# Forming the low parts of layer 1's k, q and v weights during layer 0's feed-forward and keeping them in DRAM scratch

## The chip, the cores and the metric

One core of a Trainium2 chip. The metric is the device time of one execution in microseconds; the kernel before has three runs, 1903.14, 1904.91 and 1908.84, with a median of 1904.91 us.

## The reference

One inference step of a two-layer decoder for a prompt of 512 tokens and 8 sample tokens, 520 columns in all, of width D = 1024, in float32. Layer 0 mixes with dilated-window attention and an SSM, layer 1 with a gated delta net; each is followed by a SwiGLU feed-forward of width 2816, and each of the four sub-layers stands between two RMS norms. The change is about one product, the input projection of layer 1 (8192 + 32 columns: q 1024, k 1024, v 2048, which pass a causal convolution and silu, z 2048, and gates):

```python
def gdn_mixer(h, conv_buf, s0, w_in, conv_w, dt_bias, a_log, norm_w, w_out):
    proj = h @ w_in
    qkv, z, b_raw, a_raw = jnp.split(proj, [GDN_QKV, GDN_QKV + GDN_VW, ...], axis=-1)
    qkv, new_conv = causal_conv(qkv, conv_buf, conv_w)
    qkv = jax.nn.silu(qkv.astype(f32))
    ...
    o, s_fin = gated_delta_rule(q, k, v, g, beta, s0)
    ...
def swiglu(h, w_gate, w_up, w_down):
    return (jax.nn.silu(h @ w_gate) * (h @ w_up)) @ w_down
```

The outputs also hold the updated states and caches. The sample caches come back with every row moved up by one, which the kernel does with 32 copies of 1 MB from DRAM to DRAM.

## The kernel before

**Products.** Activations lie feature-major: 128 features on the partitions, 520 tokens in two halves of 256 and 264. TensorE multiplies float32r operands, so each weight tile W is split into a high part (W rounded by a cast) and a low part (W minus the high part), and so is each activation x. A product is hi·xh + hi·xl + lo·xh: three matmuls for each 128 × 128 weight tile and token half, six for both halves (`lin`).

**Weights.** `WStream.load` brings raw weights into a ring of two buffers of 1 MB, for the input projections and feed-forward gate and up 8 row tiles × 256 columns, so two column tiles a load (the out-projection of layer 0: 12 row tiles × 128 columns, 768 KB). `WStream.split` then works in units of four row tiles × 128 columns: a cast of 128 × 512 into a buffer `whi` (L289 on ACT, L290 where DVE or POOL does it), and a subtraction into `wlo` (L165). Each of the two rings has four units. `s.lo_pool` chooses the engine of the subtraction at each stage: POOL for every unit, or for every second or third, DVE for the others.

**Order.** A scheduler decides the order of instructions on each of the five engines, with priorities; on the chip each engine then takes its own list strictly in order, and waits on semaphores. SP issues nearly all DMAs (L296), so its list is also the order in which transfers enter its queue. `copy_after` hangs one cache copy behind every `copy_every`-th weight load: every 4th in layer 0 and layer 1, none for the z columns and the output projection of layer 1, every 2nd in the last feed-forward; what is left goes at the end.

**Stages.** Layer 0's input projection and mixers; its out-projection (`w_hyb_out`; the last column tiles are computed by token halves, all first halves before the second); the boundary (residual and norm: DVE and ACT, PE works on the feed-forward's first tiles as the norm's parts arrive); feed-forward 0, whose gate and up run over 11 pairs of column tiles and down over 22 row tiles; boundary; layer 1 from about 840 us on. In layer 1, `l1` computes the gates and k tiles, the elimination systems of the delta rule, q tiles and v tiles. Each of the 32 tiles passes `conv_tile`: a scale from PSUM, four steps of a convolution (L281 `cs<-cs,cw` on DVE, others on ACT and POOL `cs<-cs,p`), silu (L281 `p<-p,cs`). The elimination (`l1_eliminate`, products `p<-p,b` and `b<-p` on DVE with both inputs in SBUF) runs between them; the scheduler mixes the two.

Names that are needed below: `raw`, `whi`, `wlo` (the rings), `cs` and `b4` (two large SBUF buffers that each stage uses for other things), `gqd0` and `gqd1` (queries of layer 1 kept in DRAM and loaded back to `b4` four at a time), `ktd` (keys kept likewise), `acc` (PSUM accumulators), `ma` and `mb` (other PSUM).

Of the kernel before, what the change touches and what calls it, by code (L numbers as in the profile page):

```python
# [28 lines left out]
EPS = 1e-6  # L29
# [91 lines left out]

def KN(n, v, *others):
    """The engine, share or order chosen at a place: v unless the table has another of the choices."""
    return KNOBS.get(n, v)
# [4 lines left out]
class WStream:  # L129
    """Weights, in the order of use: loaded in groups, split into hi + lo in units of at most 4 row tiles."""  # L130

    def __init__(s, k):
        s.k, s.ng, s.nu, s.nh = k, 0, 0, 0
        s.raw = s.key = None

# [12 lines left out]
    def split(s, raw, ko, nk, off, spread=None, out=None):  # L148
# [7 lines left out]
        with k.tc.high_priority():  # L156
# [3 lines left out]
            for o, d, n in spread or [(off, 0, 128)]:  # L160
                s.nh += 1
                k.cp("V" if k.hi_v and s.nh % k.hi_v == 0 else "A", hi[:, :nk, d:d + n], raw[:, :, o:o + n])
                s.nu += 1
# [5 lines left out]
    def tile(s, ap, c0, kts, spread=None, ncol=None, out=None):  # L169
        """Yield (row tile, hi, lo) for the 128 columns from c0 and the row tiles kts; input weights come two tiles a load.  # L170
        out = (buffer, offset) of 1024 floats for each four row tiles, to hold them apart from the ring."""
# [7 lines left out]
        for k0 in range(0, len(kts), 4):  # L179
            hi, lo = s.split(raw, kts[k0], 4, off, spread, out and out[k0 // 4])  # L180
            for j in range(4):
                yield kts[k0] + j, hi[:, j], lo[:, j]

    def rows(s, ap, c0, loads):
        """As tile() for a tall matrix; loads are (first row tile, count, unit offsets in their order)."""
# [9 lines left out]
class Ker:  # L195
# [14 lines left out]
    def gen(s, *names):  # L210
        """From here on these buffers hold something else: float32r operands and float32 data never share a tile."""
# [3 lines left out]
    def lay(s, name, off=0, n=KD, dt=F32R):  # L215
        """Operand (tile, half) -> columns, for n tiles of all tokens."""
# [3 lines left out]
    def layh(s, name, n=KD):  # L220
        """As lay(), the first half of the tokens of every tile before the second."""
# [64 lines left out]
    def cp(s, e, out, in_):  # L286
        """Copy on ACT, DVE or GpSimd."""
# [10 lines left out]
    # ---- linear layers: weights stationary, 520 token columns moving in two halves  # L298
    def lin(s, w, xh, xl, nkt, halves=(0, 1), ps=None):
        """ps[half] = sum over row tiles of w (yielding (row tile, hi, lo)) of hi'xh + hi'xl + lo'xh."""  # L300
# [7 lines left out]
    def group(s, w, xh, xl, nkt):  # L308
        """Up to four tiles, the first half of the tokens of all before the second half, which may come later."""
# [13 lines left out]
    def lnexp(s, ins):  # L323
        """After ins, one table load for Ln and Exp."""
# [1561 lines left out]
```

## Time and profile before

The profiled execution has a span of 1901.6 us; the runs are 1.5 to 7.2 us above that (median 3.3).

| stage, window in us | PE busy | DVE | ACT | POOL | granted clock |
| --- | --- | --- | --- | --- | --- |
| gate norm of layer 0 and before, 300 to 363 | 53.66 of 63 | 38.62 | 35.25 | 24.46 | 0.95 |
| out-projection of layer 0, 363 to 425 | 61.64 of 62 | 29.38 | 33.66 | 20.38 | 1.00 |
| boundary, start of feed-forward 0, 425 to 480 | 49.53 of 55 | 46.81 | 29.79 | 27.10 | 0.88 |
| feed-forward 0, 560 to 640 | 80.00 of 80 | 24.36 | 21.23 | 36.13 | 1.00 |
| layer 1, 870 to 900 | 26.66 of 30 | 26.40 | 17.41 | 19.23 | 1.00 |
| layer 1, 950 to 1000 | 30.98 of 50 | 49.58 | 26.57 | 36.13 | 0.84 |
| layer 1, 1200 to 1250 | 50.00 of 50 | 39.66 | 27.37 | 26.08 | 1.00 |

A busy PE is a TensorE that has a matmul in work; matmuls are pipelined, so this is not the same as full use. Each engine's column is the time in which it executed something. PE's clock falls where PE idles. A row of groups gives the line, the engine, the operation, output and inputs by name, shape, count, the group's busy time, the mean of one in ns, and the idle time of the engine before them with what ended it. A row of the chain gives a start, a duration and what the chain ran through there.

### The profile page before, as it was taken

How to read it: one execution, taken by the hardware profiler on the slowest of the kernel's cores; microseconds unless marked ns; L12 is line 12 of the kernel's file. 1: busy time of each engine (PE TensorE's matmuls, PEld its weight loads, DVE VectorE, ACT ScalarE, POOL GpSimd, SP SyncE). 2: the span in 40 equal slices, each digit the busy share in tenths (PEclk: the TensorE clock that was granted, in tenths of full speed). 3: DMA queues.
4: the chain of work that ended last, by engine and by line, in shares of the span. 5: the costliest groups of instructions: out<-in, count | busy, mean ns of one | idle time of the engine just before them, and what ended most of it. 6: DMA issues, size and time to landing. Idle time of an engine off the chain costs nothing.

```text
span 1901.6 us, 36269 instructions
## 1 busy us (share of the span) xinstructions
PE 1746.8 (92%) x14263; PEld 1659.2 (87%) x14263; DVE 1190.0 (63%) x2334; ACT 748.7 (39%) x1828; POOL 876.2 (46%) x768
## 2 busy tenths in 40 slices
PE   8899999898999999988968898989889999999996
PEld 7888777698999999977857787978889899999996
DVE  6898878638323221178899977888954954443125
ACT  5432335555222223355756555544334511111222
POOL 2565756234444433435474554646668411112452
PEclk9999999998999999999988899999989899999998
DMA  7345765453333334453442123257998333432333
GB/s 259 125 130 183 237 202 142 145 182 113 111 111 112 112 106 136 124 177 114 137 139 72 59 65 92 63 156 212 272 290 237 132 135 134 134 133 84 92 92 106
DMA packets 293323, 268.88 MB, mean 141 GB/s; under 512 B 11841, under 2 KB 276742, under 8 KB 291986
## 3 DMA queue, kind: packets, MB, share of 16 engines
q1 hardware_dynamic: 292502, 265.90, 45.5%
q8 instruction: 112, 1.84, 0.4%
q10 hardware_dynamic: 652, 0.68, 0.1%
q14 instruction: 57, 0.47, 0.1%
HBM read 241.01 MB, written 62.04 MB: 159 GB/s over the span
## 4 chain that ended last, share of the span: by engine, by line
PE 56%; DVE 26%; DMA 8%; issue 4%; ACT 4%; POOL 2%; SPq 1%; DVEq 0%; POOLq 0%; ACTq 0%
PE acc L268 48%; DVE p L274 4%; DVE cs L281 4%; PE ma L268 4%; PE mb L268 3%; DVE b L274 2%; DVE sq L281 2%; DMA raw<-in_w_ffn_down_dram 2%; DVE p L281 1%; DVE Hh L281 1%; PE mb L271 1%; DVE cs L274 1%; DMA bm<-csd 1%; POOL cs L274 1%; DVE wlo L165 1%
## 5 line engine op out<-in xcount | busy, mean ns | idle before, releaser
L165 POOL TENSOR_TENSOR wlo<-raw,whi 128x512 fp32r<-128x512 f32 (+3 forms) x373 | 500.8, 1346 | 676.7 <-ACT whi L289 368.1
L268 PE MATMUL acc<-Hl,whi 128*128 128x256 f32 (+1 forms) x2576 | 565.6, 291 | 20.2 <-DVE Hl L281 8.5
L268 PEld LDWEIGHTS acc<-Hl,whi 128*128 128x128 f32 x2576 | 420.5, 193 | 35.4 <-issue 11.3
L289 ACT CAST whi<-raw 128x512 fp32r<-128x512 f32 (+3 forms) x392 | 234.4, 602 | 453.0 <-PE acc L268 388.2
L268 PE MATMUL acc<-Hh,whi 128*128 128x256 f32 (+1 forms) x1824 | 387.0, 287 | 3.5 <-DVE cs L274 2.0
L268 PE MATMUL acc<-Hh,wlo 128*128 128x256 f32 (+1 forms) x1824 | 389.0, 288 | 0.0
L268 PEld LDWEIGHTS acc<-Hh,whi 128*128 128x128 f32 x1824 | 292.5, 191 | 8.2 <-issue 5.1
L268 PEld LDWEIGHTS acc<-Hh,wlo 128*128 128x128 f32 x1824 | 292.8, 191 | 7.5 <-issue 6.7
L268 PE MATMUL acc<-bm,whi 128*128 128x256 f32 (+1 forms) x1136 | 237.1, 290 | 1.4 <-DVE bm L281 1.4
L268 PE MATMUL acc<-p,whi 128*128 128x264 f32 (+1 forms) x1280 | 230.6, 287 | 4.4 <-ACT p L1819 1.6
L290 DVE CAST whi<-raw 128x512 fp32r<-128x512 f32 x131 | 61.1, 467 | 256.7 <-PE acc L268 195.2
L165 DVE TENSOR_TENSOR wlo<-raw,whi 128x512 fp32r<-128x512 f32 (+1 forms) x150 | 117.5, 785 | 142.2 <-ACT whi L289 138.8
L268 PEld LDWEIGHTS acc<-p,whi 128*128 128x128 f32 x1280 | 190.6, 192 | 6.4 <-ACT p L1819 1.9
L268 PEld LDWEIGHTS acc<-bm,whi 128*128 128x128 f32 x1136 | 182.1, 193 | 3.7 <-issue 1.6
L268 PE MATMUL acc<-p,wlo 128*128 128x256 f32 (+1 forms) x704 | 164.4, 288 | 8.7 <-DVE wlo L165 7.0
L268 PE MATMUL acc<-Hl,wlo 128*128 128x256 f32 (+1 forms) x752 | 171.1, 293 | 1.0 <-POOL wlo L165 0.9
L268 PEld LDWEIGHTS acc<-Hl,wlo 128*128 128x128 f32 x752 | 126.4, 195 | 3.2 <-POOL wlo L165 1.6
L268 PEld LDWEIGHTS acc<-p,wlo 128*128 128x128 f32 x704 | 119.6, 192 | 10.1 <-DVE wlo L165 7.9
L281 DVE SCALAR_TENSOR_TENSOR cs<-cs,cw 128x512 f32<-128x512 f32 x100 | 96.4, 966 | 12.7 <-POOL cs L274 8.6
L268 PE MATMUL acc<-X,whi 128*128 128x264 f32 (+1 forms) x512 | 100.4, 291 | 1.7 <-DVE X L274 1.3
L268 PEld LDWEIGHTS acc<-X,whi 128*128 128x128 f32 x512 | 80.4, 195 | 3.2 <-DVE X L274 1.6
L281 DVE SCALAR_TENSOR_TENSOR Hh<-cs,CS,Hh 128x256 f32<-128x256 f32 x64 | 53.1, 894 | 26.5 <-POOL Hh L274 26.2
(465 smaller groups left out, 2932.6 us busy)
## 6 DMA issues: line engine op xcount, KB each, us to landing
raw<-in_w_gdn_in_dram SPq DMA_DIRECT2D x24, 1024.0 KB
raw<-in_w_ffn_gate_dram SPq DMA_DIRECT2D x22, 1024.0 KB
raw<-in_w_ffn_up_dram SPq DMA_DIRECT2D x22, 1024.0 KB
raw<-in_w_ffn_down_dram SPq DMA_DIRECT2D x20, 1024.0 KB
raw<-in_w_hyb_in_dram SPq DMA_DIRECT2D x16, 1024.0 KB
out_sv_dram<-in_cache_attn_v_dram SPq DMA_DIRECT2D x16, 1023.0 KB
out_sk_dram<-in_cache_attn_k_dram SPq DMA_DIRECT2D x16, 1023.0 KB
raw<-in_w_gdn_out_dram SPq DMA_DIRECT2D x10, 1024.0 KB
```

The source lines that it names most:

```text
L165: eng.tensor_tensor(out=lo[:, :nk, d:d + n], in0=raw[:, :, o:o + n], in1=hi[:, :nk, d:d + n].bitcast(F32), op=ALU.subtract)
L268: s.nc.tensor.matmul(out, lhsT=lhsT, rhs=rhs, start=start, stop=stop, skip_group_check=skip)
L271: s.nc.tensor.transpose(out, in_, s.ident[0:in_.shape[0], 0:in_.shape[0]])
L274: return (eng or s.nc.vector).tensor_tensor(out=out, in0=a, in1=b, op=op).ins
L281: return s.nc.vector.scalar_tensor_tensor(out=out, in0=a, scalar=sc, in1=b, op0=op0, op1=op1).ins
L289: return s.nc.scalar.copy(out, in_).ins
L290: return (s.nc.vector if e == "V" else s.nc.gpsimd).tensor_copy(out, in_).ins
```

## The change

In the feed-forward of layer 0 a list `todo` of 60 units is set up: 30 of the 32 k, q and v column tiles of `w_gdn_in` (k tiles 2 to 7, q 0 to 7, v 0 to 15, each in two units of four row tiles). `park` takes one unit: SP loads its 256 KB of raw weights into one of two places in `cs`, ACT casts it into one of two places in `b4`, POOL subtracts in place, SP stores the 256 KB result to a scratch tile `pk0` to `pk59` in DRAM. Three units are asked for after each pair of tiles; the rest (27) after the loop. In layer 1 `split` finds such a unit by its key: the cast to `whi` stays, but `wlo` is loaded from scratch by a DMA in place of the subtraction. No cache copies are hung behind the loads of feed-forward 0; they start again with layer 1. The products themselves are the same.

```diff
+PARK = 3
+PTILES = [*range(10, 16), *range(8), *range(16, 32)]
 class WStream:
     def __init__(s, k):
         s.raw = s.key = None
+        s.parked, s.todo = {}, []
...
-    def split(s, raw, ko, nk, off, spread=None, out=None):
+    def park(s, n=1):
+        k = s.k
+        for _ in range(min(n, len(s.todo))):
+            ap, c0, k0 = s.todo.pop(0)
+            q = len(s.parked)
+            raw, lo = k.B("cs", 1040 + 512 * (q % 2), 4, 128), k.B("b4", 2080 + 512 * (q % 2), 4, 128, dt=F32R)
+            k.dma(raw, ap[k0 * 128:(k0 + 4) * 128, c0:c0 + 128].rearrange("(k p) c -> p k c", p=128))
+            k.cp("A", lo, raw)
+            k.tt(lo, raw, lo.bitcast(F32), ALU.subtract, k.nc.gpsimd)
+            d = k.dr.tile([128, 4, 128], F32, tag="pk%d" % q, name="pk%d" % q)
+            k.dma(d, lo.bitcast(F32))
+            s.parked[ap.tensor.name, ap.offset, c0, k0] = d
+
+    def split(s, raw, ko, nk, off, spread=None, out=None, low=None):
...
                 k.cp("V" if k.hi_v and s.nh % k.hi_v == 0 else "A", hi[:, :nk, d:d + n], raw[:, :, o:o + n])
+                if low is not None:
+                    k.dma(lo.bitcast(F32), low)
+                    continue
                 s.nu += 1
                 eng = nc.gpsimd if (k.lo_pool and s.nu % k.lo_pool == 0) else nc.vector
...
-            hi, lo = s.split(raw, kts[k0], 4, off, spread, out and out[k0 // 4])
+            hi, lo = s.split(raw, kts[k0], 4, off, spread, out and out[k0 // 4], s.parked.get((ap.tensor.name, ap.offset, c0, kts[k0])))
...
     def ffn(s, l):
         s.gen("p2" if l == 0 else "bm")
+        if l == 0:
+            w = s.i["w_gdn_in"][0]
+            s.copy_every = 0
+            s.W.todo = [(w, 128 * t, k0) for t in PTILES for k0 in (0, 4)]
...
                     s.tt(hl(t, h), gt, a.bitcast(F32), ALU.subtract)
+                if l == 0:
+                    s.W.park(PARK)
+        s.W.park(1000)
...
     def l1(s):
+        s.copy_every = KN('cev0', 4, 3, 5, 6)
```

In the built programs POOL has 52 subtractions of L165 fewer and 60 `b4<-cs,b4` more, DVE 8 subtractions fewer, ACT 60 casts more, SP 180 DMAs more; PE has the same instructions. Lines of the kernel are 22 further down after the change (L318 is the old L296, L187 the old L165). The scheduler puts the units not only into feed-forward 0: the first two loads stand before the end of layer 0's attention samples, units 0 to 19 are stored during the out-projection, 20 to 27 around the boundary.

SP's list in the second half of layer 0's out-projection, before (`raw` is the weight load of a column tile, `out_sv` and `out_sk` a cache copy):

```order
L296 DMA raw_4530<-in_w_hyb_out_dram 128x12x128
L296 DMA raw_4585<-in_w_hyb_out_dram 128x12x128
L296 DMA out_sv_dram<-in_cache_attn_v_dram 16x16368
L296 DMA raw_4641<-in_w_hyb_out_dram 128x12x128
L296 DMA raw_4740<-in_w_hyb_out_dram 128x12x128
```

The same place after the change, from `raw_4585` on (`cs_78` is a unit's raw weights, `pk12` its scratch tile):

```order
L318 DMA raw_4585<-in_w_hyb_out_dram 128x12x128
L318 DMA out_sv_dram<-in_cache_attn_v_dram 16x16368
L318 DMA pk12_5796<-b4_5014 128x512
L318 DMA cs_78<-in_w_gdn_in_dram 128x4x128
L318 DMA pk13_5801<-b4_5014 128x512
L318 DMA cs_78<-in_w_gdn_in_dram 128x4x128
L318 DMA raw_4641<-in_w_hyb_out_dram 128x12x128
L318 DMA pk14_5806<-b4_5014 128x512
L318 DMA cs_78<-in_w_gdn_in_dram 128x4x128
L318 DMA pk15_5877<-b4_5014 128x512
L318 DMA raw_4740<-in_w_hyb_out_dram 128x12x128
```

The weight loads of the out-projection now stand behind stores, which wait for POOL, and loads, which wait for the place in `cs`.

SP's list in feed-forward 0, before:

```order
L296 DMA raw_5538<-in_w_ffn_gate_dram 128x8x256
L296 DMA raw_5668<-in_w_ffn_up_dram 128x8x256
L296 DMA raw_5802<-in_w_ffn_gate_dram 128x8x256
L296 DMA raw_5932<-in_w_ffn_up_dram 128x8x256
L296 DMA out_sv_dram<-in_cache_attn_v_dram 16x16368
```

And after:

```order
L318 DMA raw_5597<-in_w_ffn_gate_dram 128x8x256
L318 DMA pk28_6470<-b4_5014 128x512
L318 DMA cs_78<-in_w_gdn_in_dram 128x4x128
L318 DMA pk29_6475<-b4_5014 128x512
L318 DMA cs_78<-in_w_gdn_in_dram 128x4x128
L318 DMA pk30_6678<-b4_5014 128x512
L318 DMA cs_78<-in_w_gdn_in_dram 128x4x128
L318 DMA pk31_6683<-b4_5014 128x512
L318 DMA cs_78<-in_w_gdn_in_dram 128x4x128
L318 DMA raw_5727<-in_w_ffn_up_dram 128x8x256
```

Four stores and four loads now stand between two weight loads, up to unit 59.

SP's list at the end of layer 1's v tiles, before (the last `raw` loads of v and the first of z; `gqd` are queries coming back into `b4`):

```order
L296 DMA raw_12723<-in_w_gdn_in_dram 128x8x256
L296 DMA raw_12881<-in_w_gdn_in_dram 128x8x256
L296 DMA b4_9674<-gqd0_11426 128x512
L296 DMA raw_14205<-in_w_gdn_in_dram 128x8x256
L296 DMA raw_14357<-in_w_gdn_in_dram 128x8x256
```

And after:

```order
L318 DMA raw_13171<-in_w_gdn_in_dram 128x8x256
L318 DMA wlo_13016<-pk52_7646 128x512
L318 DMA b4_9964<-gqd0_11716 128x512
L318 DMA wlo_13044<-pk53_7651 128x512
L318 DMA wlo_13094<-pk54_7854 128x512
L318 DMA wlo_13122<-pk55_7859 128x512
L318 DMA raw_14495<-in_w_gdn_in_dram 128x8x256
L318 DMA b4_9964<-gqd0_11716 128x512
L318 DMA wlo_13174<-pk56_7864 128x512
L318 DMA b4_9964<-gqd1_12059 128x512
```

The low parts of the last v tiles now stand in the same list as the loads of `b4`, and behind one of them each.

## The prediction

> **What bounds the kernel now.** I read the page first for the engine shares and the chain, then windows by stage, then PE's waits, and last the groups of DVE and POOL in the stage that the change relieves.
>
> ```profile
> span 1901.6 us, 36269 instructions
> PE 1746.8 (92%) x14263; PEld 1659.2 (87%) x14263; DVE 1190.0 (63%) x2334; ACT 748.7 (39%) x1828; POOL 876.2 (46%) x768
> PE 56%; DVE 26%; DMA 8%; issue 4%; ACT 4%; POOL 2%; SPq 1%; DVEq 0%; POOLq 0%; ACTq 0%
> ```
>
> PE is busy for 1746.8 of 1901.6 us, so all idle time of PE is 155 us; a change that leaves PE's instructions alone can win only there. DVE carries a quarter of the chain. The windows say where (columns: window, its length, busy time of PE, PEld, DVE, ACT, POOL with instruction counts, granted clock, DMA share, GB/s):
>
> ```profile
> 403.00:424.00 21.00, 21.00 (x175) 20.90 (x174) 8.81 (x13) 13.35 (x28) 7.03 (x8) 1.00 0.66 201
> 424.00:442.00 18.00, 12.84 (x79) 10.95 (x77) 17.97 (x27) 11.19 (x27) 12.49 (x11) 0.79 0.58 176
> 480.00:560.00 80.00, 80.00 (x668) 80.00 (x667) 23.80 (x51) 21.12 (x46) 35.66 (x28) 1.00 0.37 119
> 900.00:950.00 50.00, 46.29 (x379) 44.82 (x377) 43.38 (x80) 36.91 (x130) 19.84 (x17) 1.00 0.47 143
> 950.00:1000.00 50.00, 30.98 (x248) 30.45 (x249) 49.58 (x62) 26.57 (x77) 36.13 (x27) 0.84 0.40 132
> 1000.00:1050.00 50.00, 40.06 (x312) 38.94 (x312) 48.40 (x92) 31.81 (x96) 19.79 (x20) 0.92 0.26 86
> 1050.00:1100.00 50.00, 40.04 (x557) 38.05 (x556) 49.06 (x85) 27.25 (x61) 25.94 (x30) 0.86 0.14 44
> 1100.00:1150.00 50.00, 49.58 (x674) 47.15 (x674) 35.36 (x52) 30.30 (x67) 32.54 (x33) 0.96 0.23 65
> ```
>
> The feed-forward of layer 0 (480 to 560, and alike on both sides) has PE full and DVE, ACT and POOL at 30, 26 and 45%. The in-projection of layer 1 from 950 to 1100 has DVE full (147.0 of 150 us) and PE at 111.1, so 38.9 us of PE's idle time lie there. After 1100 PE is full again. What PE waits for between 840 and 1150:
>
> ```profile
> PE mb L271 <- DVE sd L274: 22.7, 2, 16.1
> PE acc L268 <- DVE cs L274: 5.1, 4, 2.0
> PE acc L268 <- POOL wlo L165: 0.6, 1, 0.6
> ```
>
> PE waits for DVE's products, and for a low part from POOL for 0.6 us only. So the subtractions that go are not themselves late; they matter through what they do to DVE.
>
> **What a subtraction on POOL costs DVE.** Two elimination products on DVE, and the POOL subtraction beside the first (start, duration):
>
> ```profile
> 977.60 1.34 POOL L165 TENSOR_TENSOR wlo<-raw,whi 128x512 fp32r<-128x512 f32 x1
> 977.83 1.28 DVE L274 TENSOR_TENSOR p<-p,b 128x135 f32<-128x135 f32 x1
> 983.78 0.31 DVE L274 TENSOR_TENSOR p<-p,b 128x156 f32<-128x156 f32 x1
> ```
>
> The larger product takes 0.31 us alone; the smaller takes 1.28 us beside the subtraction. Both of its inputs are in SBUF, as are the subtraction's. The groups between 870 and 1110 show the same in the mean, against two single rows of the chain of waits that had no POOL work beside them:
>
> ```profile
> L281 DVE SCALAR_TENSOR_TENSOR cs<-cs,cw 128x512 f32<-128x512 f32 x57 | 53.9, 950 | 3.9 <-POOL cs L274 3.4 <-ACT cs L284 0.2
> L281 DVE SCALAR_TENSOR_TENSOR p<-p,cs 128x512 f32<-128x512 f32 x16 | 14.7, 920 | 0.7 <-ACT p L284 0.7
> L165 DVE TENSOR_TENSOR wlo<-raw,whi 128x512 fp32r<-128x512 f32 x8 | 6.2, 769 | 0.6 <-ACT whi L289 0.6
> L165 POOL TENSOR_TENSOR wlo<-raw,whi 128x512 fp32r<-128x512 f32 x42 | 59.4, 1415 | 31.2 <-ACT whi L289 24.9 <-DVE whi L290 4.0 <-issue 1.8
> 902.90 0.68 DVE wlo L165
> 908.38 1.37 DVE wlo L165
> 970.21 0.60 DVE p L281
> 983.20 0.66 DVE cs L281
> ```
>
> 57 convolution steps at 0.66 would take 37.6 instead of 53.9 us, 16 at 0.60 would take 9.6 instead of 14.7: 21.4 us of excess in these two groups. Doing the same with every DVE instruction of the timeline (its time over the shortest of its own shape) and giving the excess to the POOL instruction that it overlaps most, I get 63.2 us between 870 and 1110, of which 27.6 stand beside L165's subtractions and 33.4 beside POOL's other work, which stays. Between 950 and 1110, where DVE sets the end, the L165 share is 20.5 us.
>
> On the reason: the Trainium skill (SBUF — State Buffer, Who interferes with whom) says that a DVE instruction with two SBUF inputs and a GpSimd instruction that reads SBUF exclude each other, the later one waiting for the other's whole length. The rows agree in kind (1.28 against 0.31). If every subtraction held DVE for its whole length, the gain between 870 and 1110 would be 59.4 us instead of 27.6; the rows decide, and the sum below does without this.
>
> **What goes from layer 1.** 52 POOL and 8 DVE subtractions. On DVE's stretch from 950 to 1110: 20.5 us of excess. Before 950 the chain passes to and fro between DVE, ACT, PE and small transfers, so the remaining 7.1 us of excess count as nothing and of the 8 DVE subtractions only the two rows of the chain, 0.68 + 1.37 = 2.0 us. Together 22.5. Bounds: 10 if half of the excess is taken up by POOL's other products moving into the freed time; 27.6 + 6.2 = 33.8 if all of it is on the path. Above that the 38.9 us of PE's idle time close it.
>
> **What layer 1 gets instead.** 60 loads of 256 KB from scratch into the low-part ring, on SP's queue. A 256 KB load of the same shape in the trace, and the longest one that stood in a busy queue:
>
> ```profile
> 1158.39 3.39 DMA b<-gqd
> 1173.55 3.36 DMA b<-gqd
> 258.67 8.76 DMA cs<-in_state_ssm_dram
> ```
>
> A unit of four row tiles is 24 matmuls; by the 668 matmuls in 80 us a unit lasts PE 2.9 us, and the ring holds four, so a slot that comes free is needed again three units, 8.6 us, later. 3.4 us fit in this, with 0.4 for the issue. 8.8 do not, and SP is in order: the low parts of the last v tiles now stand among loads of `b4` from `gqd`, which wait for buffers of the elimination, and the weight load behind them waits too. One such wait over the lead costs 3 to 6 us. I take 3 off the gain (0 to 8).
>
> **What layer 0 pays.** 60 times: a 256 KB load, an ACT cast, a POOL subtraction, a 256 KB store. The last two have rows in the feed-forward, and PE's chain there is one piece:
>
> ```profile
> 473.22 319.97 PE acc L268 x2662
> L165 POOL TENSOR_TENSOR wlo<-raw,whi 128x512 fp32r<-128x512 f32 x79 | 101.9, 1290 | 137.6 <-ACT whi L289 102.5 <-DVE whi L290 26.3 <-PE acc L268 8.7
> L289 ACT CAST whi<-raw 128x512 fp32r<-128x512 f32 x58 | 36.0, 620 | 133.3 <-PE acc L268 130.9 <-issue 2.4
> ```
>
> Two slots alternate, so the round of a slot gives two parks: the load, a cast of 0.62, a subtraction of 1.29 and some 0.4 us of issue. The load lands in 3.4 us on a free queue; its own slot's store stands just ahead of it, and 0.262 MB at the queue's ceiling of 305 GB/s (201 GB/s at 66% in the window from 403) are 0.86 us. So 4.25 for the landing and 6.55 for the round.
>
> In the feed-forward (parks 28 to 59, four for each of eight 1 MB weight loads): a weight load lasts PE 96 matmuls, 11.5 us, so a round may take 5.75. POOL gets 4 × 1.29 = 5.2 us more in that time on top of 35.66/80 × 11.5 = 5.1, 90% busy; ACT 21.12/80 = 26% plus 4 × 0.62/11.5 = 22%. PE hides all of it as long as the round keeps up; otherwise the weight loads behind the stores on SP, the whi casts behind the park casts on ACT and the ring's subtractions behind the parks' on POOL are late together. 16 rounds × 0.8 us = 12.8, less the 8.6 us that the ring is ahead: 4 us (0 at a landing of 3.4; 25 at a landing of 5.6).
>
> In the last part of layer 0 (parks 0 to 27) there is less cover:
>
> ```profile
> 344.84 1.28 ACT L284
> 353.48 1.28 ACT L284
> 358.56 0.70 DVE p L274
> 363.78 53.68 PE acc L268 x446
> 403.35 14.84 SPq L296 DMA_DIRECT2D raw<-in_w_hyb_out_dram  x4
> 424.57 0.98 DVE R L281
> 442.30 13.92 PE acc L268 x93
> ```
>
> - The gate norm (344 to 363) is a chain over ACT and DVE. Two casts, 1.24 us, are put into ACT's order there, and four subtractions beside DVE's products; the casts of parks 2 and 3 wait on ACT for a load and hold the norm's last casts behind them: 2 us (0 to 6).
> - The out-projection (364 to 424). Parks 0 to 19 stand in SP's order ahead of the feed-forward's first load: ten rounds in 60 us, 6.0 each, against 6.55, so 5.5 late, less about a half tile of lead (4.3 us): 1. At the tail the queue binds too: four 768 KB loads leave within 14.84 us, one every 4.8, and PE is full, because it takes these tiles in token halves at twice the usual pace. Between the loads `raw_4585` and `raw_5016`, some 21 us, SP now issues 8 stores and 8 loads of parks, 4.2 MB, 13.8 us at the ceiling, with 34% or 7.1 us free. Half of the 6.7 us over is hidden by the raw ring's second slot. Together 4 us (0 to 12).
> - The boundary to the feed-forward (424 to 442). DVE is busy for 17.97 of 18 us and PE waits for it; POOL gets about ten park subtractions, at most half of whose 13 us can fall on DVE's products (the share above, 20.5 us for about 30 subtractions, is 0.68 each). 10 × 0.68 × about half of them on the path: 3 us (0 to 7).
>
> By the same page of the Trainium skill each of these subtractions could hold a DVE product for its whole 1.29 us, 13 us at this boundary instead of 3; the time would then be 10 us above the sum below, and this is the fourth rival.
>
> **The cache copies.** The ten 1 MB copies that ran in layer 0's feed-forward are postponed; ten now stand between the two loads of layer 1's down-projection tiles. The page's DMA slices (40 of 47.5 us) have a share of 0.3 there:
>
> ```profile
> DMA  7345765453333334453442123257998333432333
> ```
>
> 1 us (0 to 7).
>
> **The sum.** −22.5 + 3 + 2 + 4 + 3 + 4 + 1 = −5.5 us (gain, late low parts, gate norm, out-projection, boundary, feed-forward, copies). Against the profiled span of 1901.6 that is 1896.1. The median of the runs shown, 1904.91, lies 3.3 above the span (start and end around it), so 1899.4; I say **1899**.
>
> **Rivals.**
> 1. *Slower: the round of two slots paces layer 0.* If a park's load lands in 5.0 us, within the rows' 3.4 to 8.8, the round is 7.3: 16 × 1.55 − 8.6 = 16 us in the feed-forward and 10 × 1.3 − 4.3 + 3 = 12 in the out-projection, 28 instead of 8, so 1919. It loses to the kernel before from a landing of about 4.5 us. For it: the queue in the feed-forward goes from 119 GB/s (0.37) to some 270, since each 11.5 us then carry 2.1 MB of parks beside a 1 MB load, 90% of the ceiling; SP, ACT and POOL are in order. Against: the 1 MB load leaves behind the parks' loads and not ahead of them.
> 2. *No change: the relief is half of what I count* (11 of 22.5), because DVE's excess moves to POOL's other products and the last v tiles are bound by PE anyway: 1911 with all costs, 1904 with half of the 14 us of layer 0 and the copies. For it: 33.4 of the 63.2 us of excess stand beside other POOL work. Against: that work does not grow.
> 3. *Faster than the sum:* all excess is on the path (33.8), and the layer-0 costs and the copies are half (7 instead of 14), with the 3 us of late low parts: −24, 1881. For it: PE's idle time would allow it. Against: the chain before 950 is mixed.
> 4. *The lock at the boundary:* 1909, within the uncertainty of the measurement.
>
> That the change does not do what it says I leave out: 60 loads of low parts stand in SP's order.
>
> **How the numbers follow.** The sum 0.42 (1893 to 1905), first rival 0.20, second 0.16, third 0.15, fourth 0.07. Faster or slower means by over 0.3%, 5.7 us, about what a measurement of this kernel can tell from no change: below 1899.2 or above 1910.6. Faster: 0.23 of the sum and 0.15 of the third, 0.38. Slower: 0.20 of the first, 0.07 of the second, 0.03 of the fourth, 0.30. Same: the remaining 0.32. The range leaves a tenth outside on each side, a part of the third rival and the longer landings of the first: **1881 to 1921**.
>
> **What would show each step.** PE's idle time in the in-projection (42.6 us in the four windows from 900 to 1100) halves; the group `cs<-cs,cw` falls from a mean of 950 to about 800 ns, and PE's waits for `sd` shrink. In the feed-forward PE stays one piece of 320 us; any wait for `wlo` or `whi` there is rival 1. PE waits for weights in the out-projection for about 4 us, and the boundary is some 3 us longer. I am wrong if the in-projection keeps its length with the excess gone (then DVE's excess was not on the path), or if the feed-forward breaks up.

## The result and the profile after

The changed kernel takes 1923.72 us (median of 5 runs, 1917.70 to 1925.14) against 1904.91 us (1903.14 to 1908.84): a ratio of 1.008, 95% interval 1.0054 to 1.0106. It is slower by 0.8%, some 15 to 19 us. The profiled execution has a span of 1923.3 us, at the upper end of its runs. One sentence of the description of the change is wrong: units are asked for three per column tile, six per pair, so the loop asks for all 60 and nothing is left behind it; where the units stand in the engines' lists is as shown.

Where the time went is read by laying the matmuls of PE side by side: start of the n-th matmul after the change minus start of the n-th before, both in order of start. PE's matmuls are the same, so the difference is time lost or won up to there (inside layer 1 the order differs a little, and only points where both stand at the same kind of matmul are used). All numbers are us.

| place, time before | after | units formed, not used | only layer 1 changed | units from the feed-forward on | paced by three | v tiles, two | two phases, 40 units | two phases, all 60 |
| --- | --- | --- | --- | --- | --- | --- | --- | --- |
| attention samples, 345 | 8.3 | 9.8 | 3.8 | 2.0 | 3.1 | 7.2 | -0.2 | 4.3 |
| in the gate norm, 379 | 14.4 | 15.8 | 4.9 | 2.0 | 3.1 | 7.1 | -0.2 | 4.3 |
| end of the out-projection, 424 | 19.4 | 20.9 | 4.9 | 2.0 | 3.1 | 7.1 | -0.2 | 4.3 |
| boundary, 463 | 22.6 | 24.6 | 5.5 | 1.0 | 2.2 | 6.4 | -2.6 | 3.3 |
| feed-forward, 476 | 30.2 | 31.9 | 5.5 | 8.1 | 8.6 | 8.6 | -2.6 | 3.3 |
| feed-forward, 572 | 43.2 | 40.4 | 5.5 | 21.9 | 12.5 | 11.8 | -2.6 | 3.3 |
| down-projection, 704 | 43.2 | 40.4 | 5.5 | 33.3 | 23.8 | 18.1 | -2.6 | 3.3 |
| boundary to layer 1, 818 | 41.3 | 40.4 | 4.0 | 33.6 | 23.7 | 17.6 | -4.1 | 1.6 |
| layer 1, 953 | 31.5 | 40.7 | -5.7 | 23.2 | 13.8 | 19.1 | 0.6 | -1.2 |
| layer 1, 1109 | 15.6 | 39.2 | -20.2 | 8.6 | -0.7 | 1.3 | -17.1 | -21.1 |
| layer 1, 1202 | 20.1 | 44.3 | -14.6 | 15.4 | 5.0 | 2.2 | -8.5 | -16.4 |
| end, 1894 | 22.0 | 43.8 | -11.9 | 17.1 | 8.2 | 8.4 | -0.8 | -11.6 |

The first column is the changed kernel, the others are the experiments below. Up to 345 the kernels that put nothing in that place scatter between -0.2 and 7.2, which is the scatter from one execution to the next; only what a column adds from row to row below that is used. The change loses 34.9 us between 345 and 704 and wins 21.2 between 818 and 1202.

The windows of the changed kernel, in the feed-forward and in layer 1 (columns as before):

```profile
417.00:445.00 28.00, 25.93 (x195) 23.89 (x194) 12.44 (x13) 16.17 (x33) 20.15 (x16) 1.00 0.92 269
480.00:560.00 80.00, 71.42 (x551) 69.61 (x550) 41.18 (x71) 33.30 (x71) 58.72 (x44) 0.94 0.62 190
560.00:640.00 80.00, 73.32 (x592) 71.43 (x591) 27.69 (x45) 28.37 (x61) 55.31 (x42) 1.00 0.59 186
640.00:720.00 80.00, 80.00 (x668) 80.00 (x667) 25.63 (x53) 21.21 (x46) 36.09 (x28) 1.00 0.30 93
894.00:950.00 56.00, 53.82 (x442) 52.68 (x441) 45.60 (x103) 36.64 (x95) 13.99 (x21) 1.00 0.65 211
950.00:1000.00 50.00, 45.79 (x364) 44.70 (x363) 41.31 (x66) 35.36 (x112) 14.14 (x12) 0.97 0.76 242
1000.00:1050.00 50.00, 40.66 (x319) 39.69 (x317) 48.73 (x76) 34.76 (x120) 20.43 (x15) 0.90 0.53 180
```

PE, which was full in the feed-forward, has 592 matmuls in 80 us instead of 668, until the last unit is stored (610); from 640 on it is full again. POOL is at 69 to 73% and the queue at 59 to 62%; between 527 and 612, where units run throughout, they are at 75% and 71%. Neither is full. The 90% that I had worked out for POOL was for a weight load every 11.5 us, and here they leave some 14 us apart. In the tail of the out-projection (417 to 445) the queue nearly is, at 92% and 269 GB/s.

What ACT waits for between 500 and 612 (the waiting instruction, what released it, us in total, times, the longest):

```profile
ACT b L311 <- DMA cs<-in_w_gdn_in_dram: 62.0, 29, 4.5
ACT whi L311 <- PE ma L290: 1.1, 2, 0.8
```

Before the change ACT waited for PE there (130.9 of 133.3 us of idle time in the row of the prediction). Now it stands for 62.0 us at the head of its list before a cast of a unit, until that unit's load has landed. The ring's casts are behind it in the same list, POOL's subtractions behind those, and PE waits for them (480 to 612):

```profile
PE acc L290 <- POOL wlo L187: 9.6, 11, 1.5
```

One turn of the chain, from SP's and ACT's lists:

```profile
569.72 0.37 SPq L318 DMA_DIRECT2D raw<-in_w_ffn_up_dram  x1
572.67 0.34 SPq L318 DMA_DIRECT2D pk<-b  x1
573.12 0.38 SPq L318 DMA_DIRECT2D cs<-in_w_gdn_in_dram  x1
...
582.99 0.38 SPq L318 DMA_DIRECT2D cs<-in_w_gdn_in_dram  x1
```

```profile
579.10 0.62 ACT L311 CAST b<-cs 128x512 fp32r<-128x512 f32 x1 [3.33 <-DMA cs<-in_w_gdn_in_dram]
581.68 0.60 ACT L311 CAST whi<-raw 128x512 fp32r<-128x512 f32 x1
```

The unit's load leaves 3.4 us after a 1 MB weight load on the same queue and lands 5.9 us after its issue; ACT has stood idle for 3.33 us when the unit's cast starts, and the ring's cast follows only 2.6 us later. The chain of waits runs from unit to unit: between 520 and 612, 58.9% of it are landings of units' loads and 12.7% units' subtractions, and PE's matmuls are 6.5%. Eight of its twelve landings, from 3.0 to 6.0 us (start, duration):

```profile
531.29 6.01 DMA cs<-in_w_gdn_in_dram
541.29 4.06 DMA cs<-in_w_gdn_in_dram
547.93 5.08 DMA cs<-in_w_gdn_in_dram
555.58 4.05 DMA cs<-in_w_gdn_in_dram
562.21 4.19 DMA cs<-in_w_gdn_in_dram
567.57 2.98 DMA cs<-in_w_gdn_in_dram
573.12 5.88 DMA cs<-in_w_gdn_in_dram
582.99 3.91 DMA cs<-in_w_gdn_in_dram
```

Of the 20.6 us that are lost between 463 and 572 in the table, 7.6 are lost before 476, and not by this chain. DVE still works there on the second token half of the boundary's norm, and its products meet the units' subtractions on POOL:

```profile
469.08 2.94 POOL L296 TENSOR_TENSOR b<-cs,b 128x512 fp32r<-128x512 f32 x2
469.33 1.53 DVE L296 TENSOR_TENSOR acc<-acc,sd 128x256 f32<-128x256 f32 x1
470.78 1.53 DVE L303 SCALAR_TENSOR_TENSOR R<-rs,rs 128x264 f32<-128x264 f32 x1
472.24 0.41 DVE L296 TENSOR_TENSOR acc<-acc,sd 128x256 f32<-128x256 f32 x1
```

```profile
PE acc L290 <- DVE Hl L303: 3.4, 3, 1.8
```

The same product takes 1.53 us beside a unit's subtraction and 0.41 us without one. DVE's excess, counted as in the prediction over the matmuls that ran from 443 to 476 before, is 11.4 us instead of 4.1, and 6.3 of it stand beside units' subtractions. The experiments below agree: where units are subtracted in this stretch the excess is 8.2 to 12.3 us and 2.2 to 7.6 us are lost between 463 and 476; those without (among them the one with the same bytes and both with two phases) have an excess of 4.0 to 4.2 us and lose nothing. No experiment takes away these subtractions alone.

In layer 1 the promised relief is there. PE's wait for DVE's `sd`, 22.7 us before, is 5.3; the excess of DVE's instructions beside L165's subtractions, counted as in the prediction but over the whole stretch up to the time 1157 of the kernel before, falls from 36.2 us to 2.7, and DVE's busy time there from 276.5 to 234.6 us. PE's idle time in the stretch falls from 53.3 to 33.2 us. The group of the convolution has a mean of 868 instead of 950 ns (what is left stands beside POOL's other products), and PE waits for DVE still:

```profile
L303 DVE SCALAR_TENSOR_TENSOR cs<-cs,cw 128x512 f32<-128x512 f32 x55 | 47.6, 868 | 4.8 <-POOL cs L296 3.4 <-ACT cs L306 1.1
PE acc L290 <- DVE cs L296: 17.1, 4, 7.7
PE mb L293 <- DVE sd L296: 5.3, 1, 5.3
```

### The profile page after: what moved, and what is told of

Same layout as the page of the kernel before. It is cut to its first block, busy times and chain, and to the rows that moved or that the text cites. A ratio compares the mean times of both kernels' runs of the same rounds, so it can differ in the third digit from the quotient of the medians.

```text
span 1923.3 us, 36684 instructions
## 1 busy us (share of the span) xinstructions
PE 1757.5 (91%) x14263; PEld 1664.6 (87%) x14263; DVE 1179.4 (61%) x2326; ACT 778.5 (40%) x1888; POOL 888.5 (46%) x776
## 4 chain that ended last, share of the span: by engine, by line
PE 49%; DVE 17%; DMA 9%; ACT 5%; issue 4%; POOL 2%; SPq 1%; DVEq 0%; ACTq 0%; POOLq 0%
PE acc L290 40%; PE ma L290 4%; DMA cs<-in_w_gdn_in_dram 4%; DVE p L296 3%; PE mb L290 2%; DVE sq L303 2%; DMA raw<-in_w_ffn_down_dram 2%; DVE cs L303 1%; POOL b L296 1%; PE mb L293 1%; DVE p L303 1%; DVE b L296 1%; DVE Hh L303 1%; ACT L306 1%; DMA b<-gqd 1%
## 5 line engine op out<-in xcount | busy, mean ns | idle before, releaser
L187 POOL TENSOR_TENSOR wlo<-raw,whi 128x512 fp32r<-128x512 f32 (+2 forms) x321 | 424.7, 1328 | 554.7 <-ACT whi L311 282.9
L290 PE MATMUL acc<-Hl,whi 128*128 128x256 f32 (+1 forms) x2576 | 565.6, 292 | 32.5 <-DVE cs L296 17.1
L312 DVE CAST whi<-raw 128x512 fp32r<-128x512 f32 x131 | 66.2, 506 | 243.6 <-PE acc L290 183.2
L187 DVE TENSOR_TENSOR wlo<-raw,whi 128x512 fp32r<-128x512 f32 (+1 forms) x142 | 118.9, 841 | 140.1 <-ACT whi L311 135.2
L290 PEld LDWEIGHTS acc<-p,wlo 128*128 128x128 f32 x704 | 119.0, 191 | 11.8 <-DVE wlo L187 9.3
L296 POOL TENSOR_TENSOR b<-cs,b 128x512 fp32r<-128x512 f32 x60 | 85.6, 1430 | 53.7 <-ACT b L311 49.5
L303 DVE SCALAR_TENSOR_TENSOR cs<-cs,cw 128x512 f32<-128x512 f32 x100 | 89.7, 898 | 14.7 <-POOL cs L296 9.7
```

The costliest lines, as they stand in the source:

```text
L187: eng.tensor_tensor(out=lo[:, :nk, d:d + n], in0=raw[:, :, o:o + n], in1=hi[:, :nk, d:d + n].bitcast(F32), op=ALU.subtract)
L290: s.nc.tensor.matmul(out, lhsT=lhsT, rhs=rhs, start=start, stop=stop, skip_group_check=skip)
L296: return (eng or s.nc.vector).tensor_tensor(out=out, in0=a, in1=b, op=op).ins
L303: return s.nc.vector.scalar_tensor_tensor(out=out, in0=a, scalar=sc, in1=b, op0=op0, op1=op1).ins
L312: return (s.nc.vector if e == "V" else s.nc.gpsimd).tensor_copy(out, in_).ins
```

## Theories

**Theory A**: two separate ledgers. Layer 1 wins about 20 us by the contention that goes; layer 0 loses about 40, because a round of the two places lasts (611.8 - 527.2) / 6 / 2 = 7.05 us (seven weight loads leave between these times, two rounds between two) where PE allows 5.75. Rivals: **B**, the bytes on the queue; **C**, POOL's or DVE's work; and that the order made by the scheduler is at fault rather than the units. Each experiment was compared with the kernel before on the same chip; that kernel's medians there were 1909.0 to 1911.5 us, so ratios are what to read.

## Experiments: the two ledgers

**Units formed but not used.**

```diff
-s.split(..., s.parked.get((ap.tensor.name, ap.offset, c0, kts[k0])))
+s.split(..., None)
```

> All 60 units are formed and stored in layer 0 as in the changed kernel, but layer 1 forms its low parts as before and does not load them. Theory A (two ledgers: layer 0 loses about 38 to 43 us because a round of the two places takes 7.0 us where PE gives 5.75, and layer 1 gains about 21 through the removed contention of POOL and DVE): 1905 + 40 = 1945, range 1938 to 1952, and layer 1 as long as before. Rival (the two parts are not separate; the loss in layer 0 is mostly a changed order of the scheduler that depends on layer 1): under 1930.

Measured: 1947.42 us, ratio 1.0195 (1.0174 to 1.0216), +37 us. Layer 1 is as before, to the wait:

```profile
PE mb L293 <- DVE sd L296: 22.8, 2, 16.2
PE acc L290 <- DVE cs L296: 5.1, 4, 2.0
```

**Only layer 1 changed.** One unit is formed, and all 60 loads read its scratch tile.

```diff
-s.W.todo = [(w, 128 * t, k0) for t in PTILES for k0 in (0, 4)]
+s.W.todo = [(w, 1280, 0)]
-s.split(..., s.parked.get(...))
+s.split(..., the one scratch tile, for the tiles in PTILES)
```

> Only one unit is formed in layer 0 and all 60 low-part loads of layer 1 read its scratch tile, so the low parts of 29 column tiles and more are not the right ones; the cache copies are placed as in the changed kernel. Theory A: the gain of layer 1 alone, 1905 - 21 = 1884, range 1878 to 1890. Rival (the gain seen in layer 1 is only slack given back because layer 0 ended late, DMAs being further ahead): within 6 us of 1905.

Measured: 1893.17 us, ratio 0.991 (0.9886 to 0.9935), -17 us. 1.0195 × 0.991 = 1.010, inside the interval of the changed kernel: the two ledgers add up. By the table some half of the gain arises before 953 (4.0 to -5.7) and the rest after it (to -14.6).

**What the loads of low parts cost.** The 30 tiles use their high part as low part: no subtraction and no load.

```diff
-lo = k.wp.tile([128, 4, 128], F32R, tag="wlo", name="wlo", bufs=4)
+lo = hi if low else k.wp.tile([128, 4, 128], F32R, tag="wlo", name="wlo", bufs=4)
```

> No units; in layer 1 the 30 tiles take their high part for the low part too, so neither a subtraction nor a load of low parts is left for them (the product is not the reference's there); cache copies as in the changed kernel. Against the kernel with one unit read 60 times (0.991) it tells what the 60 loads cost in layer 1. Theory A: 3 us less, 0.989 to 0.990. Rival (the loads cost much of the gain): 0.985 or less.

Measured: 1883.61 us, 0.987 (0.9855 to 0.9884). Between 818 and 1202 this kernel wins 25.5 us and the one with the loads 18.6, so the 60 loads cost about 7 us: between the two expectations. I had taken 3 (0 to 8).

**Is it contention?** In place of the 60 subtractions POOL fills the low-part buffer with zeros, twice for each unit; nothing is read from SBUF.

```diff
-eng.tensor_tensor(out=lo, in0=raw, in1=hi, op=ALU.subtract)
+for _ in range(2):
+    nc.gpsimd.memset(lo.bitcast(F32), 0.0)
```

> No units and no low-part loads; in layer 1 the 60 subtractions of the 30 tiles are replaced by two fills of the low-part buffer with zeros each on POOL (so the low parts of these tiles are zero). POOL is kept about as busy and PE waits for POOL as before, but these instructions read nothing from SBUF. Theory A (the gain of layer 1 is the contention between the subtractions and DVE's products with two SBUF inputs, which needs a POOL instruction that reads SBUF): about as the kernel without any low parts, 0.987 to 0.990. Rival (the gain is POOL's time or the wait for POOL): 0.997 or more.

Measured: 1890.55 us, 0.990 (0.9867 to 0.9933). POOL's group in the same stretch:

```profile
L185 POOL MEMSET wlo<- 128x512 f32 x120 | 62.1, 528 | 53.5 <-PE acc L292 46.4 <-PE ma L292 5.2
```

POOL is at work on low parts for 62.1 us of this stretch; the subtractions before took

```profile
L165 POOL TENSOR_TENSOR wlo<-raw,whi 128x512 fp32r<-128x512 f32 x56 | 79.7, 1426 | 46.9 <-ACT whi L289 39.5 <-DVE whi L290 5.1 <-issue 1.8
```

The excess on DVE beside these instructions is 8.2 us instead of 36.2, 0.13 us for each us of POOL instead of 0.45. The kernel gains 20.8 us in the medians and 17.0 us between 818 and 1202 by the method of the table, where the one without any low parts gains 27.9 and 25.5. So two thirds to three quarters of the gain are there with POOL at work for 152.7 us of this stretch (165.2 before): for that part it is neither POOL's time nor the wait for it, but that the subtraction reads SBUF. Whether the rest is POOL's time or scatter is open. This is what the Trainium skill (SBUF — State Buffer, Who interferes with whom) states of a GpSimd instruction that reads SBUF and one that only writes it. Its exclusive lock agrees with the single row of the prediction: the product that starts at 977.83 ends at 979.11, 0.17 us after the subtraction. The 36.2 us beside 56 subtractions of 1.426 us are 0.65 us each, not quite half an instruction; that is a mean over all of them, also those that met no such product.

## Experiments: what costs layer 0 its time

**Units from the feed-forward on.** The loads are queued behind the feed-forward's first weight loads.

```diff
+with k.tc.issue_after(the last weight load ahead of the loop):
     k.dma(raw, ap[...])
```

> All 60 units, none queued before the first loads of the feed-forward, then as densely as the scheduler puts them (four for each weight load). Theory A: the out-projection and the boundary are as before, but 28 rounds at 7.0 us instead of 16 stand in the feed-forward: 28 x 1.25 - 8.6 = 26 us lost there, 1905 - 21 + 26 = 1910, range 1902 to 1918; between the changed kernel and the paced one. Rival (the loss is made by the units in the out-projection and at the boundary): 1888.

Measured: 1920.79 us, 1.0055 (1.0035 to 1.0075). Gate norm, out-projection and boundary lose nothing now (2.0 to 1.0 in the table), but the feed-forward loses 32.3 us instead of 20.6: 7.1 up to 476, beside the norm, and 25.2 after it, where 28 rounds were expected to cost 26. Four units for each weight load do not fit, wherever they start.

**Three units for each weight load.**

```diff
+with k.tc.issue_after(k.last_load):
     k.dma(raw, ap[...])
 ...
+            if l == 0 and p:
+                s.W.park(PARK)      # after the gate tiles of a pair, and again after the up tiles
```

> All 60 units as in the changed kernel, but each unit's load is queued behind the weight load current at that time, three units for each 1 MB weight load of layer 0's feed-forward from its second pair of tiles on, none before. Theory A: 1.5 rounds of 7.0 us are 10.5 us against the 11.5 us that PE takes for a weight load, so the units are hidden: 1905 - 21 + 2 = 1886, range 1880 to 1894. Rival B (the loss comes from the number of bytes on the queue or from POOL's work, not from the round): part of the loss stays, over 1898.

Measured: 1910.03 us, 0.9995 (0.9975 to 1.0015). Theory A failed here: 1.5 rounds of 7.05 us would be hidden, and yet 21.6 us are lost in the feed-forward, 6.4 of them up to 476 and 15.2 after it. The chain of this kernel:

```profile
605.07 0.49 SPq L319
605.65 6.14 DMA cs<-in_w_gdn_in_dram
611.86 0.62 ACT b L312
612.48 0.53 ACT whi L312
...
613.81 0.64 POOL wlo L188
615.25 1.29 POOL b L297
616.54 1.26 POOL wlo L188
617.82 0.37 SPq L319
618.28 6.70 DMA cs<-in_w_gdn_in_dram
```

A weight load leaves at 605.07, a unit's load behind it lands 6.1 us later, ACT casts it and then a ring unit, POOL does unit, ring, unit, ring, and only then is the raw buffer free for the next weight load: 12.7 us, where PE takes 11.5. I took the loop to be closed by POOL, where ring and units alternate (theory A2).

**The same bytes without the chain.** Loads and stores at four of each for each weight load, no casts and subtractions; layer 1 as before.

```diff
-k.cp("A", lo, raw)
-k.tt(lo, raw, lo.bitcast(F32), ALU.subtract, k.nc.gpsimd)
```

> The 60 loads and 60 stores of the units at the density of the kernel that starts them in the feed-forward (four of each for each weight load), but without cast and subtraction (two casts only, the stores write the same two places again and again), and layer 1 forms its low parts as before. So the same bytes on SP's queue without the chain over ACT and POOL. Theory A: what is lost in layer 0 falls from the 33 us of that kernel to under 8: at most 1.004. Rival B (bytes): a loss of about 30 us, 1.015.

Measured: 1908.43 us, 0.998 (0.9963 to 0.9997). PE is not held up for a moment:

```profile
480.00:560.00 80.00, 80.00 (x668) 80.00 (x667) 25.18 (x54) 22.05 (x49) 36.14 (x28) 1.00 0.88 271
476.49 319.95 PE acc L292 x2662
```

At 271 GB/s and 88% of the queue the feed-forward is one piece of 320 us, as before the change. Rival B is out.

**Ring subtractions on DVE.** The paced kernel with POOL left to the units.

```diff
-s.lo_pool = KN("lp_f%d" % l, 1, 2, 3)
+s.lo_pool = KN("lp_f%d" % l, 1, 2, 3) if l else 0
```

> The paced kernel (three units for each weight load), and in gate and up of layer 0's feed-forward the weight ring's own subtractions go to DVE instead of POOL. Theory A2 (in the paced kernel the weight loads wait for the ring's subtractions, these stand behind the units' subtractions in POOL's order, those wait for a unit's load, and that load lands 6 us after issue because it is queued behind the weight load: a loop of 12.5 us against the 11.5 of PE): without the ring's subtractions on POOL the loop is open, the units are hidden, and the time is 0.991 to 0.993 of the kernel before (-14 to -17 us). Rival B (bytes on the queue): as the paced kernel, 1.000. Rival C (DVE's subtractions collide with the units' on POOL and DVE then holds PE): over 1.000.

Measured: 1907.39 us, 0.999 (0.9979 to 1.0). The feed-forward still loses (9.9 at 476, 20.7 at 704), so POOL alone did not close the loop. With the ring's subtractions off POOL, ACT remained.

**Fewer units.** The v tiles only, two units for each weight load, one round in 11.5 us.

```diff
-PARK = 3
+PARK = 2
-PTILES = [*range(10, 16), *range(8), *range(16, 32)]
+PTILES = [*range(16, 32)]
```

> Only the 16 v tiles (32 units), two for each weight load. Theory A2: one round per weight load, 7 us against 11.5, fully hidden in the feed-forward; the gain in layer 1 is the part that arises from 950 us on, about 9 to 13 of 18.5 us: 0.993 to 0.996. Rival (any unit whose load is queued behind a weight load delays the ring, however few they are): 0.998 or more.

Measured: 1907.72 us, 0.999 (0.9975 to 1.0005). One round of 7 us in 11.5 still costs 9.5 us between 476 and 704, so here it is not the length of the round. ACT between 500 and 720:

```profile
ACT b L312 <- DMA cs<-in_w_gdn_in_dram: 76.4, 24, 8.9
ACT whi L312 <- PE acc L291: 39.8, 19, 4.5
```

24 waits for a load, up to 8.9 us: each is at the head of ACT's list, with the ring's casts behind.

**Theory A3** after this: where the round fits, what delays PE is that ACT, in order, comes to a unit's cast before the load has landed. Two ways to take this away, both with 40 units and two for each weight load. The first has the casts on POOL, and the ring's subtractions on DVE, so that nothing of the ring is behind a unit:

```diff
-k.cp("A", lo, raw)
+k.cp("G", lo, raw)
-PTILES = [*range(10, 16), *range(8), *range(16, 32)]
+PTILES = [*range(4), *range(16, 32)]
```

> 40 units (the 16 v tiles and q tiles 0 to 3), two for each weight load, their casts on POOL instead of ACT, and the weight ring's own subtractions in gate and up of layer 0's feed-forward on DVE. So neither ACT nor the weight ring is behind a unit's load any more. Theory A3 (what delays PE is the wait for a unit's load, 5 to 6 us after its issue, at the head of ACT's order, with the ring's casts behind it): nothing lost in layer 0, 0.991 to 0.993 of the kernel before. Rival (POOL's and DVE's collisions, or the waits on SP): 0.997 or more.

Measured: 1907.48 us, 0.9987 (0.9969 to 1.0005). The feed-forward loses nothing any more (8.3 at 476 and at 704), only 4.8 us at its start (3.5 at 463), where the norm's products meet the units on POOL. But layer 1 gives 6.4 us instead of the 16 that I expected for these 40 units.

The second leaves the engines as they were and asks for cast, subtraction and store one weight load later than for the load:

```diff
     def park(s, n=1):
+        for key, q, raw, lo in s.pend:          # the units loaded one step ago
+            with k.tc.issue_after(s.cast):      # behind the ring's last cast on ACT
+                k.cp("A", lo, raw)
+            ... subtract, store
```

> The same 40 units, two for each weight load, all engines as in the changed kernel (cast on ACT, subtractions on POOL), but cast, subtraction and store of a pair are asked for one weight load after its loads, so that the load has landed some 11 us before ACT comes to the cast. Theory A3: as the same number of casts no longer waits, the feed-forward is one piece and only the gain of layer 1 is left: 0.991 to 0.993. Rival (POOL's in-order list, with the units' subtractions between the ring's, is what delays PE): 0.997 to 1.000.

Measured: 1904.6 us, 0.997 (0.9954 to 0.9986). ACT's wait for loads is nearly gone, and the feed-forward is whole:

```profile
ACT b L318 <- DMA cs<-in_w_gdn_in_dram: 6.8, 9, 1.5
ACT whi L318 <- PE acc L297: 89.2, 42, 4.5
470.61 328.12 PE acc L297 x2730
```

Same engines, same bytes per unit, 76.4 us of ACT's waiting (in the kernel with the v tiles) gone to 6.8, nothing lost (-2.6 at 463 and at 704): together with the kernel that casts on POOL, this shows theory A3 for two units to a weight load. (Subtraction and store are later too here, so the units' subtractions also miss the norm.) For four, as in the changed kernel, a pair of rounds is longer than PE's 11.5 us in any case; no run has four units to a weight load in two phases. The ratio missed the expectation because of the gain in layer 1, which is 4.4 us (-4.1 to -8.5) instead of 16; the units left out are those of the k tiles and of q tiles 4 to 7, and by the table this kernel wins nothing up to 953, where the changed kernel, the one with only layer 1 changed and the two before with all units win 9.7 to 10.4. That it gives back 8.6 us between 1109 and 1202 and 7.7 after that is not explained; one wait of PE for DVE of 7.9 us between 1290 and 1400, 3.9 before, is all that the waits show.

**All 60 units in two phases**, the last of them in the down-projection:

```diff
     def rows(s, ap, c0, loads):
             raw = s.load(ap, k0, n, c0, 128)
+            if n == 16 and (s.todo or s.pend):
+                s.park(PARK)
```

> All 60 units in two phases: two units' loads for each weight load of gate and up of layer 0's feed-forward, as before, and two for each 16-row-tile load of its down-projection, each pair's cast, subtraction and store asked for one step later. Theory A3: nothing lost in layer 0 up to the down-projection's end, 0 to 3 us at the boundary to layer 1 (the last stores stand there), and the whole gain of layer 1 (18.5 to 21 us, as in the kernel with one unit read 60 times): 0.990 to 0.993 of the kernel before, the first that is clearly faster with all low parts formed. Rival (the last units' chain delays the boundary or the first k tiles, as the units did at the other boundary): 0.995 to 1.000.

Measured: 1888.06 us against 1909.01, ratio 0.9881 (0.9861 to 0.9902): 21 us faster than the kernel before, and faster than the changed kernel by 2%. Nothing is lost up to the down-projection (4.3 at 345, 3.3 at 704), 5.5 us at the boundary to layer 1 (1.6 at 818, 7.1 at 852), and layer 1 gives its whole gain, 18.0 us between 818 and 1202. The feed-forward is whole:

```profile
560.00:640.00 80.00, 80.00 (x669) 80.00 (x668) 30.42 (x51) 29.09 (x61) 55.00 (x42) 1.00 0.57 182
476.52 323.55 PE acc L299 x2692
ACT b L320 <- DMA cs<-in_w_gdn_in_dram: 10.7, 13, 1.6
```

POOL is at 69% and the queue at 57%, not far below the changed kernel's 75% and 71% between 527 and 612, and PE is full.

## Why the prediction was wrong, step by step

- **What bounds the kernel, and the gain of layer 1**: right in kind and in sum. Forecast 22.5 less 3 for late low parts, 19.5; the table gives 21.2 for the changed kernel and 18.6 with layer 1 alone. The parts were wrong. "The remaining 7.1 us of excess count as nothing" before 950: this stretch gave 9.8 us of the gain, though its chain passes between engines. The 20.5 us after 950 gave 15.9 up to 1109, of which 4.5 were given back by 1202; the loads cost about 7. PE's idle time did not halve (53.3 to 33.2 us), and the convolution's group fell to 868 ns, not to 800.
- **Gate norm**, 2 (0 to 6): 6.1 us (8.3 to 14.4), and as much (6.0) in the kernel that forms units and does not use them; nothing in those that start later. This is the upper end of its bounds.
- **Out-projection**, 4 (0 to 12): 5.0 us. It held.
- **Boundary**, 3 (0 to 7): this step failed. 3.2 us are lost up to 463, and 7.6 more up to 476, 10.8 in all. The step ended at 442, and the second token half of the norm was put at nothing, without a reason. DVE's excess rises by 7.3 us just there (4.1 to 11.4), and PE loses as much there, so all of it is on the path, where the prediction took half of 6.8 us.
- **Feed-forward**, 4 (0 to 25): this step failed in size. Between 463 and 572, 20.6 us are lost (22.6 to 43.2), the 7.6 of the norm and 13.0 after 476. The 13.0 are the mechanism that the step describes, a round that is too long, inside its bounds; the round is what was mis-sized, 7.05 us instead of 6.55. "4.25 for the landing": the eight rows above have a mean of 4.5 us and reach 6.0; cast, subtraction and issue, with the waits between them, take the other 2.55 instead of 2.30. In the eight steps from weight load to weight load between 498.3 and 611.8, each takes 14.2 us where PE takes 11.5, so the loads fall 21.5 us behind. Less "the 8.6 us that the ring is ahead" this is 12.9, and 13.0 is measured, which agrees with a lead of that size. The prediction named the lists ("the whi casts behind the park casts on ACT") and did its sum as if they mattered only when the round's mean is too long. The kernel with one round in 11.5 us loses 9.5 us and shows that they can matter without that; the changed kernel's 13.0 need no such term, but no run separates the two there.
- **The first rival** (a landing of 5.0 us, 1919 us, chance 0.20) is right in kind, the round paces layer 0, and its time is within 5 us; the latter is partly luck. The landing is 4.5 us and not 5.0, the round costs 13.0 in the feed-forward and not 16, and the out-projection loses 5.0 and not 12; the norms, which it left as they were, make up for it. Its argument against itself was wrong: "the 1 MB load leaves behind the parks' loads and not ahead of them" (569.72 and 573.12 above). Its argument for itself, 90% of the queue, was no cause either: the kernel with the same bytes and no chain had 88% and lost nothing.
- **Copies**, 1 (0 to 7): 1.9 us between 1202 and the end.
- **Not seen**: the two loads that stand among layer 0's attention samples. The two kernels with them are 8.3 and 9.8 us late at 345, the others -0.2 to 7.2; some 5 us may be theirs, but no run separates this from the scatter.
- **The lock at the boundary**, fourth rival: 13 us instead of 3 were near the 10.8 measured, one token half later than it was placed. Its time of 1909 has neither the longer round nor the gate norm in it.

The span of 1923.3 is 27 us above the sum of 1896.1: 9.0 from the round in the feed-forward (13.0 instead of 4), 7.8 from the boundary (10.8 instead of 3), 4.1 from the gate norm, 1.0 from the out-projection, 0.9 from the copies, less 1.7 from the larger gain of layer 1: 21.1. The rest is the 8.3 us up to 345, less 1.9 won between 704 and 818.

## What to carry to other kernels

A side chain of load, cast, subtraction and store is hidden only if its round fits into the time that the main path leaves for it, and if no engine on the main path comes to an instruction that waits for the chain. What matters for the second is how long ago the load was issued when the engine comes to it; the mean load of engines and queue does not show it. Asking for the later steps one weight load after the load, at the same rate, turned a loss of 9.5 us (at 32 units) into none (at 40). And look at what an instruction off the path does to the engine on it: taking 60 subtractions from POOL and DVE was worth some 20 us in layer 1 although PE had waited for them for 0.6 us, and 7.6 us were lost where such subtractions stand beside a norm on DVE.

## What was not expected of the hardware

- The queue carried 271 GB/s, 88% busy, beside a PE that was full for 320 us, with no effect on PE (80.00 of 80 us).
- Fills on POOL that only write SBUF cost DVE 8.2 us in 62.1 us of their time; subtractions that read it cost 36.2 in 79.7.
- A gain on an engine's busy time is not the gain of the stage: DVE lost 42 us of busy time in layer 1 (276.5 to 234.6) and the stage became 21 us shorter.
